# S5's rotation table begun right behind its angles, its powers doubled on POOL, the first scan two tiles earlier in the order

## The chip, the cores and the metric

The kernel runs on one core of a Trainium2 chip. The metric is the device time of one launch in microseconds. Before the change it is 912.65 us, the median of three runs (909.97 to 914.98).

The engines that matter here: TensorE (PE) does the matmuls, VectorE (DVE) and GpSimd (POOL) do elementwise work, ScalarE (ACT) does activations and copies, SyncE's queue (SP, SPq) issues all DMAs. Each engine takes its instructions strictly in the order in which the program lists them. An instruction that waits holds everything behind it on its engine.

## The reference, cut to what matters

A trunk of two layers over 512 positions of width 1024. Layer 0 is a hybrid: one input projection feeds S5 channel groups and Mamba-2 SSD heads, whose outputs are gated, concatenated and projected back. Layer 1 is a retention layer. The change is in layer 0's S5 part.

```python
def s5_mixer(u, lam_re, lam_im, log_dt, b, c, d_skip, glu_w, glu_b):   # 64 groups, 64 complex states, 16 channels
    dt = exp(log_dt); mag = exp(min(lam_re, -1e-4) * dt)
    ab = mag * (cos(lam_im * dt) + 1j * sin(lam_im * dt))       # one decay and one angle for each state
    coef = (ab - 1) / lam
    bb = coef * b
    # over all positions:  x[t] = ab * x[t-1] + bb @ u[t]
    y = real(c @ x) + d_skip * u
    y = gelu(y);  return y * sigmoid(y @ glu_w + glu_b)
# beside it, from the same projection: xbc -> silu(depthwise conv of 4 taps) -> chunked SSD scan, chunks of 128
# y = concat(y_s5 * silu(z_a), rmsnorm(y_ssd * silu(z_b))) @ w_out + residual
```

## The kernel before, in words

**Layout.** Activations stand transposed, channels on 128 partitions, the 512 positions along the free axis. A projection tile is 128 output channels: PE sums over 8 blocks of the input. Tiles before x3 use plain float32 (`mm1`, L214, or L249 for the first two). From x3 on a weight tile is split into a high and a low part (`split_w`: ACT copies the high part at L107, DVE subtracts to get the low part at L108), and PE makes three products for each block (`mm3`, L115 to L117). So each such tile needs DVE's L108 before its first L117. Tiles x0 to x11 are the SSD input: ACT L354 and three DVE instructions at L357 do the conv out of PSUM, ACT L359 the SiLU. Tiles u are S5's input, z the gates. The sums stand in three PSUM buffers, so a tile waits until the one three back has been read out.

**S5.** The recurrence is cut into blocks of 8 positions (64 blocks, `NK`). Four stages j = 0..3 hold 16 groups each.
- `s5_params` (order entry `q0`) works on [128, 64] parameters: `exp_parts` of log dt, then dt, lr, a second `exp_parts`, the angles `th` (L595 to L600), sine and cosine of half the angle (`sin_cos`), the first power `pw` (L607, L612), the coefficients `cf` (L613 to L628), powers 1 to 8 by three doublings on DVE (`cmul` at L634, six instructions each), `al` = powers times coefficients (L640), copies of the powers for the outputs (`pws`, ACT L649 and L651) and the DRAM copy `al_d` (L655). Last comes the **rotation table** `rot`: DVE makes six levels of angles and their sines and cosines (tile `s5lv`, L669 to L679), then POOL doubles the table from 1 to 64 columns (L682 to L691): seven complex products of six POOL instructions, at L534 to L539, with products in `s5rt` and sums in `rot`.
- `s5_setup` (also in `q0`) builds `bd` on POOL (`s5cm`, L716 and L717; `s5bd`, L720).
- `s5_state` (`g`) makes the input matrices from `al_d` and `b` (tiles `al`, `b`, `tm`; DVE, or POOL for the pairs in `POOL_P`, L742 to L746). `s5_scan` (`a`): 64 PE matmuls (L755), then on DVE a rotation into the scan frame (L767, L768, L770, reading `rot`), the scan itself (L772), and the rotation back (L775, L777, L782).
- `s5_kern` (`b`) makes output products O on POOL (L798 eight times and L802 four times for each j) from the powers, and stores them (`o_d`, L803). `s5_taps` (`k`) multiplies them by `bd` on PE (L814) and stores the taps. `s5_out` (`c`) gives the output.

**What sets the order.** `ORDER` is a list of stages written by hand: d steps, e decay, q S5 parameters, w the split of the input, x conv tiles, u and z projection tiles, s and t the SSD chunks, and l g a b k c for S5. At build time a planner gives every engine its order: among the instructions whose inputs are ready in its own estimate of time it takes the lowest priority number, and numbers rise in the order in which the program is traced, so in the order of `ORDER`. `rank(v)` overrides the number: -3,000,000 for the start of layer 0, -2,000,000 for weight splits (`rank_w`), -1,000,000 for work that reads PSUM out (`rank_e`). `issue_after(ins)` puts what is traced within it behind `ins` on that engine. Tiles take one of a fixed number of buffers of their tag (`m`: 20, `f`: 8); an instruction whose tile finds none free waits for the last reader of the tile that holds one.

Of the kernel before, what the change touches and what calls it, by code (L numbers as in the profile page):

```python
# [35 lines left out]
ORDER = """d0 x8 x10 x9 e0 x11 q0 x0 b0 x1 x2 w0 l0 g0 x3 x4 x5 x6 k0 b1 a0 x7 g1 s0 u2 u3 l1 t0 s1 z0 a1 z1 k1 b2 t1 s2 u4 c0 u5
# [12 lines left out]
def trunk_kernel(ctx: ExitStack, tc: tile.TileContext, a: dict, out: bass.AP):  # L49
# [481 lines left out]
    def cmul(eng, o, x, y, shape, name, conj_tmp):  # L531
        (orr, oi), (xr, xi), (yr, yi) = o, x, y
        t1, t2 = conj_tmp
        eng.tensor_tensor(t1, xr, yr, op=ALU.mult)  # L534
# [4 lines left out]
        eng.tensor_tensor(oi, t1, t2, op=ALU.add)  # L539

    def s5_params(pr):
        W = 64
# [27 lines left out]
        def sin_cos(hh, qq, zz, th, n):  # L570
            vec.tensor_scalar(hh[:, 0], th, 0.5, None, op0=ALU.mult)
            vec.scalar_tensor_tensor(n, hh[:, 0], -1.0, hh[:, 0], op0=ALU.mult, op1=ALU.max)
            vec.tensor_scalar(hh[:, 1], n, -1.0, 0.5 * math.pi, op0=ALU.mult, op1=ALU.add)
            vec.tensor_tensor(zz, hh, hh, op=ALU.mult)
            vec.tensor_scalar(qq, zz, 1.0 / math.factorial(13), None, op0=ALU.mult)
# [55 lines left out]
        for n_ in (1, 2, 4):  # L631
            base = pw[:, n_ - 1, :, :]
            sh_ = [P, n_, W]
            cmul(vec, (pw[:, n_:2 * n_, 0, :], pw[:, n_:2 * n_, 1, :]),  # L634
                 (pw[:, 0:n_, 0, :], pw[:, 0:n_, 1, :]),
                 (base[:, 0, :].unsqueeze(1).broadcast_to(sh_), base[:, 1, :].unsqueeze(1).broadcast_to(sh_)),
                 sh_, "pw", (cm1[:, 0:n_, :], cm2[:, 0:n_, :]))
# [2 lines left out]
        cmul(vec, (al[:, :, 0, :], al[:, :, 1, :]),  # L640
             (pw[:, :, 0, 32:64], pw[:, :, 1, 32:64]),
             (cf[:, 0, 32:64].unsqueeze(1).broadcast_to(sb), cf[:, 1, 32:64].unsqueeze(1).broadcast_to(sb)),
             sb, "al", (cm1[:, :, 0:32], cm2[:, :, 0:32]))
# [14 lines left out]
        vec.tensor_tensor(m8, mag[:, 0:32], mag[:, 0:32], op=ALU.mult)  # L658
        for _ in range(2):
            vec.tensor_tensor(m8, m8, m8, op=ALU.mult)  # L660
        rot = big("rot", [P, 2, 32, NK])
        pool.memset(rot[:, 0, :, 0:1], 1.0)
        pool.memset(rot[:, 1, :, 0:1], 0.0)
        lvs = t("m", "s5lv", n=384).rearrange("p (n i w) -> p n i w", i=2, w=32)
        NL = 6
        sl = [P, NL, 32]
        ang, cnt_, sc, q2 = (f(f"s5lv{i}", [P, 2, NL, 32]) for i in range(4))
        th_, n_ = ang[:, 0], cnt_[:, 0]
        for i in range(NL):  # L669
            vec.tensor_scalar(th_[:, i], th[:, 0:32], 8.0 * 2 ** i, None, op0=ALU.mult)  # L670
        vec.tensor_scalar(n_, th_, 0.5 / math.pi, MAGIC, op0=ALU.mult, op1=ALU.add)
        vec.tensor_scalar(n_, n_, MAGIC, None, op0=ALU.subtract)
        for cst in (TWO_PI_1, TWO_PI_2, TWO_PI_3):
            vec.scalar_tensor_tensor(th_, n_, -cst, th_, op0=ALU.mult, op1=ALU.add)
        sin_cos(sc, q2, cnt_, th_, n_)
        sh, ch = q2[:, 0], q2[:, 1]
        vec.scalar_tensor_tensor(lvs[:, :, 1], sh, 2.0, ch, op0=ALU.mult, op1=ALU.mult)  # L677
        vec.scalar_tensor_tensor(n_, sh, -2.0, sh, op0=ALU.mult, op1=ALU.mult)
        vec.tensor_scalar(lvs[:, :, 0], n_, 1.0, None, op0=ALU.add)  # L679
        n = 1  # L680
        rt = f("s5rt", [P, 2, 32, 16])
        while n < NK:  # L682
            lv = lvs[:, n.bit_length() - 1]
            for k0 in range(0, n, 16):
                nn = min(16, n - k0)
                sh = [P, 32, nn]
                cc, cs_ = (lv[:, i].unsqueeze(2).broadcast_to(sh) for i in range(2))
                xr, xi = (rot[:, i, :, k0:k0 + nn] for i in range(2))
                yr, yi = (rot[:, i, :, n + k0:n + k0 + nn] for i in range(2))
# [461 lines left out]
```

## Time and profile before

| what | value |
|---|---|
| median of three runs | 912.65 us (909.97 to 914.98) |
| profiled execution, device time | 915.33 us |
| its span, first to last instruction | 913.6 us |
| PE busy / granted clock, mean | 868.6 us (95%) / 0.975 |
| DVE busy | 542.5 us (59%) |
| ACT busy | 359.5 us (39%) |
| POOL busy | 229.3 us (25%) |

The span is what the trace covers; the device time has 1.7 us more around it. A busy PE isn't a PE at its peak, and a mean share says little of one stage: layer 0's early part, up to about 330 us, has other limits than the rest.

### The profile page before, as it was taken

How to read it: one execution, taken by the hardware profiler on the slowest of the kernel's cores; microseconds unless marked ns; L12 is line 12 of the kernel's file. 1: busy time of each engine (PE TensorE's matmuls, PEld its weight loads, DVE VectorE, ACT ScalarE, POOL GpSimd, SP SyncE). 2: the span in 40 equal slices, each digit the busy share in tenths (PEclk: the TensorE clock that was granted, in tenths of full speed). 3: DMA queues.
4: the chain of work that ended last, by engine and by line, in shares of the span. 5: the costliest groups of instructions: out<-in, count | busy, mean ns of one | idle time of the engine just before them, and what ended most of it. 6: DMA issues, size and time to landing. Idle time of an engine off the chain costs nothing.

```text
span 913.6 us, 11520 instructions
## 1 busy us (share of the span) xinstructions
PE 868.6 (95%) x4348; PEld 683.1 (75%) x4348; DVE 542.5 (59%) x922; ACT 359.5 (39%) x572; POOL 229.3 (25%) x187
## 2 busy tenths in 40 slices
PE   8999955989989899999999999999999999999996
PEld 4345744757768787888888888888888888888885
DVE  6978769894883466453444544655633644448445
ACT  4323344425216444433434244345411244254432
POOL 0069997170572500000013122201000303110020
PEclk9999977979999899999999999999999999999999
DMA  7386313756549636773543221221332221222322
GB/s 244 122 223 210 106 51 119 204 161 205 148 124 323 215 104 190 255 238 107 208 141 112 93 93 47 93 92 47 99 103 99 93 91 47 93 70 70 116 70 93
DMA packets 64184, 121.45 MB, mean 133 GB/s; under 512 B 18112, under 2 KB 28672, under 8 KB 64000
## 3 DMA queue, kind: packets, MB, share of 16 engines
q1 hardware_dynamic: 64128, 120.71, 41.2%
q8 instruction: 34, 0.56, 0.2%
q14 instruction: 22, 0.18, 0.1%
HBM read 103.61 MB, written 17.07 MB: 132 GB/s over the span
## 4 chain that ended last, share of the span: by engine, by line
PE 68%; DVE 12%; POOL 8%; DMA 5%; SPq 2%; issue 2%; ACT 1%; ACTq 0%; POOLq 0%; DVEq 0%
PE g L115 3%; PE qk L117 3%; PE qk L116 3%; PE g L117 3%; PE g L116 3%; PE qk L115 3%; PE v L930 3%; PE v L931 3%; PE v L929 3%; PE gl L116 2%; PE gl L117 2%; PE gl L115 2%; PE out L117 2%; PE oa L116 2%; PE oa L117 2%
## 5 line engine op out<-in xcount | busy, mean ns | idle before, releaser
L903 POOL TENSOR_TENSOR rt<-rt,ru 128x512 f32<-128x512 f32 x16 | 27.2, 1721 | 134.7 <-DVE ru L902 134.7
L972 POOL TENSOR_TENSOR os<-os,os 128x512 f32<-128x512 f32 x12 | 15.5, 1292 | 139.8 <-ACT os L970 106.9
L882 POOL TENSOR_TENSOR hs<-hs,hs 128x512 f32<-128x512 f32 x7 | 12.0, 1708 | 92.5 <-ACT hs L880 92.5
L798 POOL TENSOR_TENSOR O<-ct,s5pws 128x512 f32<-128x512 f32 x16 | 24.1, 1508 | 31.2 <-DMA ct<-in_s5c_dram 31.2
L405 ACT ACTIVATE dec<-dec,nacs 128x128 f32<-128x128 f32 x64 | 19.5, 388 | 29.3 <-DMA dec<-at_d 29.3
L902 DVE TENSOR_TENSOR ru<-qk,tab 128x512 f32<-128x512 f32 x16 | 10.9, 683 | 32.4 <-PE qk L117 32.4
L357 DVE SCALAR_TENSOR_TENSOR cva<-xbc,cvw,cva 128x511 f32<-128x511 f32 (+2 forms) x36 | 26.6, 740 | 4.3 <-ACT cva L354 4.0
L798 POOL TENSOR_TENSOR ot<-ct,s5pws 128x512 f32<-128x512 f32 x16 | 28.1, 1756 | 0.0
L802 POOL TENSOR_TENSOR O<-O,ot 128x512 f32<-128x512 f32 x16 | 27.3, 1736 | 0.0
L742 POOL TENSOR_TENSOR tm<-al,b 128x512 f32<-128x512 f32 x6 | 9.0, 1513 | 57.3 <-DMA b<-in_s5bP_dram 34.2
L461 POOL TENSOR_TENSOR za6r<-za6r,y 128x512 f32<-128x512 f32 x1 | 1.3, 1297 | 80.9 <-DMA h_d<-hb 80.9
L359 ACT ACTIVATE cva<-cva 128x512 f32<-128x512 f32 x12 | 7.6, 631 | 33.7 <-DVE cva L357 33.6
L1004 DVE TENSOR_TENSOR h<-h,out 128x512 f32<-128x512 f32 x8 | 5.5, 686 | 25.5 <-PE out L117 25.5
L1065 POOL TENSOR_TENSOR fin<-fin,fnw 128x512 f32<-128x512 f32 x4 | 5.1, 1301 | 58.7 <-ACT fq L1029 58.7
L535 POOL TENSOR_TENSOR s5rt<-rot,s5lv 128x512 f32<-128x512 f32 (+4 forms) x7 | 5.9, 837 | 50.7 <-DVE s5lv L677 50.7
L845 PE MATMUL Y<-T,U 128*64 128x128 f32 x128 | 17.4, 294 | 0.2 <-issue 0.2
L499 DVE TENSOR_TENSOR hb<-ob,hb 128x512 f32<-128x512 f32 x8 | 5.5, 689 | 20.1 <-PE ob L117 20.1
L528 DVE TENSOR_TENSOR h<-oa,h 128x512 f32<-128x512 f32 x8 | 5.5, 690 | 19.6 <-PE oa L117 19.6
L848 ACT ACTIVATE ysb<-Y 128x256 f32<-128x256 f32 x16 | 5.2, 379 | 30.2 <-PE Y L845 18.1
L844 PE MATMUL Y<-Or,X 128*64 128x128 f32 x64 | 13.7, 298 | 2.3 <-DMA Or<-o_d 2.3
L120 ACT ACTIVATE rh<-rt 128x512 fp32r<-128x512 f32 (+1 forms) x16 | 9.1, 577 | 16.9 <-POOL rt L903 16.9
L425 PE MATMUL y<-ident,yos 128*128 128x128 f32 x48 | 12.2, 339 | 3.8 <-DVE yos L399 3.8
(1726 smaller groups left out, 3012.4 us busy)
## 6 DMA issues: line engine op xcount, KB each, us to landing
al<-al_d SPq DMA_DIRECT2D x8, 512.0 KB
b<-in_s5bP_dram SPq DMA_DIRECT2D x8, 512.0 KB
dec<-at_d SPq DMA_DIRECT2D x8, 512.0 KB
o_d<-O SPq DMA_DIRECT2D x16, 256.0 KB
T<-kd SPq DMA_DIRECT2D x64, 64.0 KB
Or<-o_d SPq DMA_DIRECT2D x16, 256.0 KB
x<-in_xT_dram SPq DMA_DIRECT2D x8, 256.0 KB
u_d<-us SPq DMA_DIRECT2D x8, 256.0 KB
```

The lines of the kernel that those rows point to most:

```text
L115: pe.matmul(ps, wh[:, k, :], xh[k], start=start and i == 0, stop=False)
L116: pe.matmul(ps, wh[:, k, :], xl[k], start=False, stop=False)
L117: pe.matmul(ps, wl[:, k, :], xh[k], start=False, stop=stop and i == len(ks) - 1)
L357: vec.scalar_tensor_tensor(g[:, d:], ps[:, 0:SEQ - d], cvw[:, m, j:j + 1], g[:, d:], op0=ALU.mult, op1=ALU.add)
L405: act.activation(dec[:, i, :], dec[:, i, :], AF.Abs, bias=nacs[:, c, 8 * gr + i:8 * gr + i + 1])
L798: pool.tensor_tensor(x.rearrange("p (g k c) -> p g k c", g=4, c=16), ct[:, c, par, 4 * hf:4 * hf + 4].unsqueeze(2).broadcast_to(sh), pws[: ...
L802: pool.tensor_tensor(o, o, tm, op=ALU.add)
L845: pe.matmul(dst, U[:, 8 * par + 4 * hf + i, :], Tp[hf][:, 2 * i + par, :], start=False, stop=True)
L903: pool.tensor_tensor(t1, t1, t2, op=op)
L929: pe.matmul(ps[c], hh[kk][:, cs], wh[:, i, :], start=kk == 0, stop=False)
L930: pe.matmul(ps[c], hh[kk][:, cs], wl[:, i, :], start=False, stop=False)
L931: pe.matmul(ps[c], hl[kk][:, cs], wh[:, i, :], start=False, stop=kk == KD - 1)
```

## The change

The table's code is moved ahead of the coefficients into a function of its own, called as soon as the angles and the first power are written; its instructions are the same. The three doublings of the powers and `al` go from DVE to POOL, with rank -900,000. The first `exp_parts` gets rank -3,500,000. The products of `s5_kern` are put behind the table's last instruction on POOL. In `ORDER`, `b0` goes from before `x1` to behind `x4`, `a0` from behind `x6` to between `x5` and `x6`, and `k0 b1` behind `g1`. `sin_cos` takes the engine as an argument and is given DVE in both calls.

```diff
-ORDER = """d0 x8 x10 x9 e0 x11 q0 x0 b0 x1 x2 w0 l0 g0 x3 x4 x5 x6 k0 b1 a0 x7 g1 s0 u2 u3 ...
+ORDER = """d0 x8 x10 x9 e0 x11 q0 x0 x1 x2 w0 l0 g0 x3 x4 b0 x5 a0 x6 x7 g1 k0 b1 s0 u2 u3 ...
@@ s5_params
-        sf, em = exp_parts(pr[:, 2, :])
+        with rank(-3500000):
+            sf, em = exp_parts(pr[:, 2, :])
...
         vec.tensor_scalar(pw[:, 0, 0, :], nr, 1.0, None, op0=ALU.add)
+        def rotation():
+            m8 = sv.tile([P, 32], F32, name="s5m8")
...
+            rot = big("rot", [P, 2, 32, NK])
...
+            for i in range(NL):
+                vec.tensor_scalar(th_[:, i], th[:, 0:32], 8.0 * 2 ** i, None, op0=ALU.mult)
...
+            sin_cos(vec, sc, q2, cnt_, th_, n_)
...
+            while n < NK:
...
+                    last = cmul(pool, (yr, yi), (xr, xi), (cc, cs_), sh, "rot", (rt[:, 0, :, 0:nn], rt[:, 1, :, 0:nn]))
+                n *= 2
+            return m8, rot, last.ins
+
+        m8, rot, rot_last = rotation()
         den, t1, t2 = s(), s(), s()
...
-            cmul(vec, (pw[:, n_:2 * n_, 0, :], pw[:, n_:2 * n_, 1, :]),
+            with rank(-900000):
+                cmul(pool, (pw[:, n_:2 * n_, 0, :], pw[:, n_:2 * n_, 1, :]),
...
-        cmul(vec, (al[:, :, 0, :], al[:, :, 1, :]),
+        with rank(-900000):
+            cmul(pool, (al[:, :, 0, :], al[:, :, 1, :]),
...
-        m8 = sv.tile([P, 32], F32, name="s5m8")
...
-                cmul(pool, (yr, yi), (xr, xi), (cc, cs_), sh, "rot", (rt[:, 0, :, 0:nn], rt[:, 1, :, 0:nn]))
-            n *= 2
@@ s5_kern
-                for c, x in enumerate((o, tm)):
-                    pool.tensor_tensor(x.rearrange("p (g k c) -> p g k c", g=4, c=16),
...
+                with tc.issue_after(s5["rot_last"]):
+                    for c, x in enumerate((o, tm)):
+                        pool.tensor_tensor(x.rearrange("p (g k c) -> p g k c", g=4, c=16),
...
                 pool.tensor_tensor(o, o, tm, op=ALU.add)
```

## Rows read from the trace of the kernel before

**Rows 1.** Stretches: length, busy time of PE, PEld, DVE, ACT, POOL, granted clock, DMA.
```profile
101.00:124.30 23.30, 23.30 (x174) 18.75 (x172) 12.77 (x14) 6.64 (x10) 22.44 (x19) 1.00 0.29 94
124.30:161.00 36.70, 17.44 (x55) 12.53 (x55) 35.98 (x37) 19.68 (x40) 30.41 (x18) 0.72 0.32 101
...
127.80:138.00 10.20, 4.12 (x9) 2.88 (x10) 10.20 (x15) 8.32 (x24) 10.20 (x8) 0.50 0.01 2
...
148.30:158.50 10.20, 4.78 (x11) 3.79 (x12) 10.08 (x8) 1.53 (x3) 6.41 (x4) 0.50 0.35 114
```
**Rows 2.** Waits of PE, 0 to 330 us: total, times, longest.
```profile
PE z L117 <- DVE z0l L108: 7.8, 1, 7.8
PE u L115 <- DVE cva L357: 5.2, 1, 5.2
PE u L117 <- DVE u3l L108: 4.2, 1, 4.2
```
**Rows 3.** Waits of DVE, 84 to 161 us.
```profile
DVE gi L767 <- POOL rot L536: 4.2, 1, 4.2
DVE X L768 <- POOL rot L539: 2.8, 1, 2.8
...
DVE xbc7l L108 <- ACT xbc7h L107: 1.7, 1, 1.7
```
**Rows 4.** Wait of ACT at the second scan's mg, 84 to 161 us.
```profile
ACT mg L760 <- POOL s5rt L538: 12.3, 1, 12.3
```
**Rows 5.** POOL in order of time, the table's first and last instruction: start, duration.
```profile
52.76 0.35 POOL L535 TENSOR_TENSOR s5rt<-rot,s5lv 128x32 f32<-128x32 f32 x1 [50.71 <-DVE s5lv L677]
...
122.98 1.30 POOL L539 TENSOR_TENSOR rot<-s5rt 128x512 f32<-128x512 f32 x1
```
**Rows 6.** POOL's busy time on the table (tile rot), then on bd (tile s5cm).
```profile
50.00:125.00 75.00, 35.41 (x42) 1.00 0.55 166
...
50.00:95.00 45.00, 0.00 (x0) 13.14 (x16) 1.00 0.72 212
```
**Rows 7.** POOL's busy time on the output products, L798, then on L802.
```profile
50.00:125.00 75.00, 15.82 (x9) 1.00 0.55 166
...
50.00:125.00 75.00, 5.40 (x4) 1.00 0.55 166
```
**Rows 8.** POOL's busy time on the table's products of 64, 128 and 256 elements.
```profile
59.00:89.50 30.50, 2.75 (x6) 1.00 0.72 226
90.00:95.45 5.45, 3.35 (x6) 1.00 0.24 81
95.50:100.65 5.15, 4.88 (x6) 1.00 0.26 91
```
**Rows 9.** DVE in order of time: the first power, xn.
```profile
23.02 0.19 DVE L612 TENSOR_SCALAR s5pw<-s5scr 128x64 f32<-128x64 f32 x1
...
25.72 4.91 DVE L255 TENSOR_TENSOR xn<-x,rbc 128x512 f32<-128x512 f32 x8
```
**Rows 10.** DVE's and POOL's busy time on the table's levels (tile s5lv).
```profile
39.00:54.00 15.00, 8.07 (x25) 0.62 (x2) 1.00 0.54 147
```
**Rows 11.** DVE line 121, POOL idle, then busy: min/median/max ns, first to last start.
```profile
L121 DVE TENSOR_TENSOR xl<-xn,xh x4: 680/681/682, 32.9 to 34.7; 128x512 fp32r<-128x512 f32 x4
...
L121 DVE TENSOR_TENSOR xl<-xn,xh x4: 692/1213/1639, 78.2 to 85.7; 128x512 fp32r<-128x512 f32 x4
```
**Rows 12.** PE in order of time: dt, the last taps' matmuls, half the first scan's.
```profile
26.47 7.04 PE L294 MATMUL dt<-xn,dtw 128*16 128x512 f32 x16 [1.42 <-DVE xn L255]
...
107.46 1.09 PE L814 MATMUL K<-O,s5bd 128*32 128x128 f32 x24
...
114.39 1.90 PE L755 MATMUL S<-U,al 128*64 128x64 f32 x32
```
**Rows 13.** SP in order of time: a weight load.
```profile
93.75 0.33 SPq L98 DMA_DIRECT2D u2w<-in_w_u_dram  x1
```
**Rows 14.** ACT in order of time: that weight tile's first use.
```profile
108.09 1.04 ACT L107 ACTIVATE u2h<-u2w 128x1024 fp32r<-128x1024 f32 x1
```

More of the change, by code (lines that the diff above doesn't have):

```diff
@@ L35 @@
 VEC_X = ((0, 0), (1, 0), (0, 1), (1, 1))
[L36 removed]
+ORDER = """d0 x8 x10 x9 e0 x11 q0 x0 x1 x2 w0 l0 g0 x3 x4 b0 x5 a0 x6 x7 g1 k0 b1 s0 u2 u3 l1 t0 s1 z0 a1 z1 k1 b2 t1 s2 u4 c0 u5
  t2 l2 g2 s3 z2 a2 z3 k2 b3 t3 u6 c1 u7 z4 l3 g3 z5 n0 z6 a3 z7 c2 n1 z8 k3 r0 z9 z10 r1 c3 z11 p0 p1 z12 p2 z13 p3 o0 o1 z14
@@ L538, in cmul @@
         eng.tensor_tensor(t2, xi, yr, op=ALU.mult)
-        eng.tensor_tensor(oi, t1, t2, op=ALU.add)
+        return eng.tensor_tensor(oi, t1, t2, op=ALU.add)
     def s5_params(pr):
@@ L568, in exp_parts, with sin_cos @@
             return sf, em
[L570 to L575, printed above, removed]
+        def sin_cos(eng, hh, qq, zz, th, n):
+            eng.tensor_scalar(hh[:, 0], th, 0.5, None, op0=ALU.mult)
+            eng.scalar_tensor_tensor(n, hh[:, 0], -1.0, hh[:, 0], op0=ALU.mult, op1=ALU.max)
+            eng.tensor_scalar(hh[:, 1], n, -1.0, 0.5 * math.pi, op0=ALU.mult, op1=ALU.add)
+            eng.tensor_tensor(zz, hh, hh, op=ALU.mult)
+            eng.tensor_scalar(qq, zz, 1.0 / math.factorial(13), None, op0=ALU.mult)
             for k in (11, 9, 7, 5, 3):
                 sg = 1.0 if (k // 2) % 2 == 0 else -1.0
-                vec.scalar_tensor_tensor(qq, qq, sg / math.factorial(k), zz, op0=ALU.add, op1=ALU.mult)
-            vec.scalar_tensor_tensor(qq, qq, 1.0, hh, op0=ALU.add, op1=ALU.mult)
-        sf, em = exp_parts(pr[:, 2, :])
+                eng.scalar_tensor_tensor(qq, qq, sg / math.factorial(k), zz, op0=ALU.add, op1=ALU.mult)
+            eng.scalar_tensor_tensor(qq, qq, 1.0, hh, op0=ALU.add, op1=ALU.mult)
+        with rank(-3500000):
+            sf, em = exp_parts(pr[:, 2, :])
         dt = s()
@@ L601, in s5_params @@
         hh, zz, qq = (scr2[:, i].rearrange("p (i w) -> p i w", w=W) for i in range(3))
-        sin_cos(hh, qq, zz, th, n)
+        sin_cos(vec, hh, qq, zz, th, n)
         sh, ch = qq[:, 0], qq[:, 1]
@@ L612, in s5_params @@
         vec.tensor_scalar(pw[:, 0, 0, :], nr, 1.0, None, op0=ALU.add)
+        def rotation():
+            m8 = sv.tile([P, 32], F32, name="s5m8")
+            vec.tensor_tensor(m8, mag[:, 0:32], mag[:, 0:32], op=ALU.mult)
+            for _ in range(2):
+                vec.tensor_tensor(m8, m8, m8, op=ALU.mult)
+            rot = big("rot", [P, 2, 32, NK])
+            pool.memset(rot[:, 0, :, 0:1], 1.0)
+            pool.memset(rot[:, 1, :, 0:1], 0.0)
+            lvs = t("m", "s5lv", n=384).rearrange("p (n i w) -> p n i w", i=2, w=32)
+            NL = 6
+            sl = [P, NL, 32]
+            ang, cnt_, sc, q2 = (f(f"s5lv{i}", [P, 2, NL, 32]) for i in range(4))
+            th_, n_ = ang[:, 0], cnt_[:, 0]
+            for i in range(NL):
+                vec.tensor_scalar(th_[:, i], th[:, 0:32], 8.0 * 2 ** i, None, op0=ALU.mult)
+            vec.tensor_scalar(n_, th_, 0.5 / math.pi, MAGIC, op0=ALU.mult, op1=ALU.add)
+            vec.tensor_scalar(n_, n_, MAGIC, None, op0=ALU.subtract)
+            for cst in (TWO_PI_1, TWO_PI_2, TWO_PI_3):
+                vec.scalar_tensor_tensor(th_, n_, -cst, th_, op0=ALU.mult, op1=ALU.add)
+            sin_cos(vec, sc, q2, cnt_, th_, n_)
+            sh, ch = q2[:, 0], q2[:, 1]
+            vec.scalar_tensor_tensor(lvs[:, :, 1], sh, 2.0, ch, op0=ALU.mult, op1=ALU.mult)
+            vec.scalar_tensor_tensor(n_, sh, -2.0, sh, op0=ALU.mult, op1=ALU.mult)
+            vec.tensor_scalar(lvs[:, :, 0], n_, 1.0, None, op0=ALU.add)
+            n = 1
+            rt = f("s5rt", [P, 2, 32, 16])
+            while n < NK:
+                lv = lvs[:, n.bit_length() - 1]
+                for k0 in range(0, n, 16):
+                    nn = min(16, n - k0)
+                    sh = [P, 32, nn]
+                    cc, cs_ = (lv[:, i].unsqueeze(2).broadcast_to(sh) for i in range(2))
+                    xr, xi = (rot[:, i, :, k0:k0 + nn] for i in range(2))
+                    yr, yi = (rot[:, i, :, n + k0:n + k0 + nn] for i in range(2))
+                    last = cmul(pool, (yr, yi), (xr, xi), (cc, cs_), sh, "rot", (rt[:, 0, :, 0:nn], rt[:, 1, :, 0:nn]))
+                n *= 2
+            return m8, rot, last.ins
+        m8, rot, rot_last = rotation()
         den, t1, t2 = s(), s(), s()
@@ L633, in s5_params @@
             sh_ = [P, n_, W]
[L634 to L637 removed]
+            with rank(-900000):
+                cmul(pool, (pw[:, n_:2 * n_, 0, :], pw[:, n_:2 * n_, 1, :]),
+                     (pw[:, 0:n_, 0, :], pw[:, 0:n_, 1, :]),
+                     (base[:, 0, :].unsqueeze(1).broadcast_to(sh_), base[:, 1, :].unsqueeze(1).broadcast_to(sh_)),
+                     sh_, "pw", (cm1[:, 0:n_, :], cm2[:, 0:n_, :]))
         al = f("s5al", [P, 8, 2, 32])
         sb = [P, 8, 32]
[L640 to L643 removed]
+        with rank(-900000):
+            cmul(pool, (al[:, :, 0, :], al[:, :, 1, :]),
+                 (pw[:, :, 0, 32:64], pw[:, :, 1, 32:64]),
+                 (cf[:, 0, 32:64].unsqueeze(1).broadcast_to(sb), cf[:, 1, 32:64].unsqueeze(1).broadcast_to(sb)),
+                 sb, "al", (cm1[:, :, 0:32], cm2[:, :, 0:32]))
         pws = sv.tile([P, 2, 8, 2, 32], F32, name="s5pws")
@@ L656, in s5_params @@
                              al[64 * h + 8 * jp:64 * h + 8 * jp + 8].rearrange("p k c f -> p (k c) f"))
-        m8 = sv.tile([P, 32], F32, name="s5m8")
[L658 to L689, printed above, removed]
-                cmul(pool, (yr, yi), (xr, xi), (cc, cs_), sh, "rot", (rt[:, 0, :, 0:nn], rt[:, 1, :, 0:nn]))
-            n *= 2
-        return dict(pws=pws, al_d=al_d, cf=cf, m8=m8, rot=rot)
+        return dict(pws=pws, al_d=al_d, cf=cf, m8=m8, rot=rot, rot_last=rot_last)
     def s5_setup(s5):
```

6 lines of the change are left out of this document (3 added, 3 removed).

## The prediction, made before the kernel was run

> **What bounds the kernel now.** I read the page's slices first: PE is busy in 95% of the span and has its holes in layer 0, before about 330 us. The waits of PE there name the largest: 5.2, 4.2 and 7.8 us, all ended by DVE [rows 2]. A table of stretches puts a price on their place. From 101 to 124.3 us PE is never idle while DVE works 12.77 of 23.30 us; from 124.3 to 161 us DVE works 35.98 of 36.70 and PE only 17.44 [rows 1]. So PE loses 36.70 - 17.44 = 19.3 us in a stretch whose bound is DVE, right behind a stretch in which DVE idles for 23.30 - 12.77 = 10.5 us. The waits of DVE say why it idles: 4.2 and 2.8 us at L767 and L768, the first scan's products, for the rotation table on POOL, and 1.7 us twice for ACT's half of a weight split (one of the two stands) [rows 3]. ACT too stands 12.3 us, since mg needs the buffer of the table's levels [rows 4]. The reader should see one cause: the table ends at 122.98 + 1.30 = 124.3 [rows 5], and what DVE could not do before comes in one heap behind it. The table is late because POOL starts it at 52.8 [rows 5] and spends 71.5 us, only 35.4 of them on it; 13.1 go to bd [rows 6] and 15.1 + 5.4 to the first output products (of the 15.82 us of L798 the ninth, 0.76 us, is the next stage's) [rows 7].
>
> PE pays once more: behind these waits its granted clock is 0.50, the 1.2 GHz level, from 127.8 to 138.0 and from 148.3 to 158.5, where it is busy 4.12 and 4.78 us [rows 1]. At the 2.4 GHz level that work would take half: 2.1 and 2.4 us less.
>
> **The change part by part.**
>
> *The table earlier.* The table's 25 DVE instructions on its levels cost 8.07 us [rows 10] and can begin behind the angles, well before the first power at 23.0 [rows 9]. Until xn at 25.7 DVE has no idle time, but the doublings leave it and the coefficients step behind, which I estimate frees 3 us. Then come xn (to 30.6) [rows 9], the scaled inputs and splits; 5 us of levels remain, so POOL gets them at about 38. The bounds are 33.5 (all hidden before) and 52.8 (the planner leaves the levels where they are). The rank of the first exp_parts moves the chain by 2 us at most and is worth nothing by itself, since PE is busy with u1 meanwhile.
>
> *POOL's sum.* The powers are 24 instructions of the shapes of the table's own levels: 2.75 + 3.35 + 4.88 us, and 4.88 for al, 15.9 in all [rows 8]. The first 11 start with the first power at 23.2 [rows 9] and are over by about 34; al needs the coefficients and falls beside the table, say 4.9 us. The table's 35.4 with its gaps of 1.5 us then ends at 38 + 36.9 + 4.9 = 80 with bd behind it, at 93 with bd's 13.1 within it. Bounds: 33.5 + 36.9 = 70, and 52.8 + 36.9 + 4.9 + 13.1 = 108, or 119 if the first 11 us of powers also stand in front. The output products follow, 20.5 us: their end is 101 to 114.
>
> *The first scan.* Its 64 matmuls stood at 108.5 and 114.4 on PE [rows 12]; in front of x6 and x7 they come at about 95 to 104, an estimate: one to two tiles earlier, a tile being some 6 us here (from the taps' 108.5 to the scan's 114.4). The table is there by then, so DVE's two waits go: -7.0 us, each one microsecond off the DVE-bound stretch. The scan's work now also fills the two waits of 1.7 us: -3.4 (bounds 0 and -4.2, all that is left of the idle 11.25 us from 101 to 161). What is late next is DVE itself: its 48.75 us of work in that stretch, 12.77 + 35.98 [rows 1], stays. PE keeps 19.3 - 10.4 = 9 us of waits.
>
> *The clock.* With about half the waits gone I take back one of the two slow stretches: -2.4, bounds 0 and -4.5.
>
> *Powers on POOL.* DVE loses 24 small instructions, 6 us if one takes 0.25 (the first power, of the smallest size, takes 0.19 [rows 9]). It loses them before the convs, where PE's own dt and x tiles cover DVE: 0 us; without that cover, the 6. Against it, POOL now works beside xn, which feeds dt's matmuls. The row: a split of xn's size takes 0.681 us with POOL idle, 1.213 in the median with POOL busy [rows 11]. Eight times 0.53 would put xn's end at 34.9, and dt's last pair of matmuls (7.04 / 8 = 0.88 us) [rows 12] 2.3 us late. Bounds 0 and +2.3; I take +1.0, since POOL has only nine products left to run by then. The Trainium skill, in "SBUF — State Buffer", section "Who interferes with whom", speaks against this edit: a VectorE instruction with two SBUF inputs and a GpSimd one that reads SBUF exclude each other, and the later blocks fully. The slowest row, 1.639, agrees with a full block. By that rule the term would be the whole 2.3 and the sum 1.3 smaller.
>
> *Products held, order changed.* Behind the first held product stand the rest of stage 0's products, then the taps on PE and the stores on SP's queue. Before, PE ran the taps until 108.5 [rows 12] without a wait. Now k0 stands behind x7, at about 117 on PE (where the scan's matmuls ended before, 114.39 + 1.90 = 116.3 [rows 12]), with products there from 101 to 114: 0 us, bounds 0 and (119 + 20.5) - 117 = +22. The stores come as much later in a queue that also holds weight loads; those run 108.09 - 93.75 = 14 us ahead of their use [rows 13, 14], so I take 0 there.
>
> The sum: -7.0 - 3.4 - 2.4 + 1.0 = -11.8 us. The profiled execution took 915.33 us, 913.6 of it span and 1.7 around it, so it would take 903.5. It is 2.7 above the median; on the median I say 900.9, rounded 901.
>
> **The rivals.**
>
> *PE gets everything back.* If the planner puts PE's own needs (the splits, the last conv) ahead of scan work on DVE, the stretch becomes PE-bound: -19.3 - 4.5 + 1.0, so 890. For it: in 101 to 124.3 all of DVE's work, needs and some of the rest, is 12.77 us beside 23.3 of PE [rows 1], and the scan's last pieces may run later. Against it: DVE hardly idles for the 36.7 us behind, and its order is fixed from an estimate.
>
> *No change.* The table isn't the only thing late: PE stands for the taps, or DVE's queue for something else, as long as it does now. A taps wait of 12 us, products at 129, would do it: 912. For it: POOL carries 16 us more and has no slack in the sum's upper half. Against it: the sum has the products 15 us earlier.
>
> *Slower.* The levels stay where they are, powers and bd stand before the table, and it ends at 119. The scan then sits on DVE in front of x6's and x7's convs and holds them: 119 - 104 = 15 us, which PE feels from u2 on; products end at 139.5, and the taps, which these waits have pushed to about 132, hold PE another 7.5. That is 22.5 of waits, and of the 19.3 of now I would keep some 4 for DVE's heap, since DVE can work it off meanwhile: +7, and with xn +8, so 920. It decides at a table end of about 108, where products at 128.5 cost PE the 12 us just won. For it: the planner did leave the levels behind conv and dt work. Against it: DVE's powers, ahead of the levels now, are gone, and 20.5 us of products can no longer come between.
>
> **How the numbers follow.** Forecast 0.48 (895 to 907), PE gets everything back 0.17, no change 0.19, slower 0.16. A change of 0.5%, 4.6 us, is about what can be told from none here: faster lies below 908.1, slower above 917.2. Faster: nearly all of the first two, 0.65; same: the third and a little of the others, 0.21; slower: 0.14. The range of 889 to 917 leaves out the best part of the second case (0.06) and the fourth (0.14). The likeliest case's own range is 895 to 907.
>
> **What would show it.** The table's first product at about 38 and its last at 80 to 93; no wait of DVE for `rot` and none of ACT at mg; the powers on POOL from 23 to about 34 and xn over 4.9 us by at most 4; scan matmuls ahead of x6; PE's waits between 101 and 161 at about 9 us, all by DVE; one slow-clock stretch fewer; no PE wait at the taps. I am wrong if the table ends by 95 and PE still waits 15 us or more there, if PE waits for O at the taps, or if a loss as large appears past 161.

## The result, and the profile after

The change made the kernel slower: 925.83 us, the median of 4 runs (921.6 to 926.82), 1.0132 times the time before [1.0088, 1.0176]; the same kernel run again gave 925.75 and 1.0157 [1.0135, 1.0179]. The forecast was 901 (889 to 917). A trace is one execution: the one before took 915.33 us, and the medians of five later groups of runs of it, 109 in all, lay at 909.7 to 912.6. So medians say by how much, and traces where.

Two stretches of the changed kernel, which answer to the first two of [rows 1]; columns as there.

```profile
101.00:124.30 23.30, 18.26 (x113) 15.03 (x114) 23.30 (x24) 3.23 (x6) 23.30 (x15) 0.87 0.46 130
124.30:161.00 36.70, 27.05 (x123) 19.98 (x123) 35.02 (x39) 24.50 (x46) 26.00 (x17) 0.79 0.34 114
```

DVE now works 23.30 of 23.30 us where it had worked 12.77, and as long as before behind it: 58.3 us in place of 48.75. PE, which had been full up to 124.3, now loses time there. The waits of PE from 0 to 330 us, changed kernel, against [rows 2]:

```profile
PE Y L852 <- DMA Or<-o_d: 11.0, 4, 4.1
PE xbc L115 <- DVE cva L357: 7.0, 2, 3.5
PE z L117 <- DVE z0l L108: 4.0, 1, 4.0
PE z L115 <- DVE cva L357: 3.8, 1, 3.8
...
PE S L762 <- DVE al L753: 1.5, 1, 1.5
```

Of the old waits at u 0.5 us is left, and that at z0 has halved. New are those for the convs of x tiles. Those for the loads Or, all past 200 us, are 11.0 where the same view of before has 2.5.

POOL in order of time, changed kernel (start, duration): the table's first product, the first power, the last of al, the table's last, against [rows 5].

```profile
40.62 0.27 POOL L535 TENSOR_TENSOR s5rt<-rot,s5lv 128x32 f32<-128x32 f32 x1 [39.06 <-DVE s5lv L635]
...
41.80 0.29 POOL L534 TENSOR_TENSOR s5cm<-s5pw 128x64 f32<-128x64 f32 x1
...
75.03 0.72 POOL L539 TENSOR_TENSOR s5al<-s5cm,s5cm 128x256 f32<-128x256 f32 x1
...
100.06 2.14 POOL L539 TENSOR_TENSOR rot<-s5rt 128x512 f32<-128x512 f32 x1
```

The levels came in time and the table ends 22 us earlier, at 102.2. But POOL stood idle for 39 us, while the first power was ready at 23.9 (DVE, L613): the powers are queued behind the table's first product, step by step between its products. al is done at 75.8; on DVE it was done at 41.1. al goes through DRAM into the first stage's input matrices (P0). DVE in order of time, kernel before: P0's first and last product with the first pair of its second half between them, and the convs of x3 and x4.

```profile
64.55 0.93 DVE L742 TENSOR_TENSOR tm<-al,b 128x512 f32<-128x512 f32 x1
...
71.75 1.27 DVE L742 TENSOR_TENSOR tm<-al,b 128x512 f32<-128x512 f32 x2
...
76.99 0.68 DVE L746 TENSOR_TENSOR al<-al 128x512 f32<-128x512 f32 x1
...
93.64 2.30 DVE L357 SCALAR_TENSOR_TENSOR cva<-xbc,cvw,cva 128x511 f32<-128x511 f32 x3
...
99.25 2.30 DVE L357 SCALAR_TENSOR_TENSOR cva<-xbc,cvw,cva 128x511 f32<-128x511 f32 x3
```

P0 stood between the steps of convs there too (x11's took from 63.9 to 71.2), but among the plain tiles, and PE lost nothing from 54.7 to 124. The same in the changed kernel: the conv of x2, that of x3 with P0's second half (its first half began at 90.41), and that of x4.

```profile
87.35 0.73 DVE L357 SCALAR_TENSOR_TENSOR cva<-xbc,cvw,cva 128x511 f32<-128x511 f32 x1
...
92.92 0.73 DVE L357 SCALAR_TENSOR_TENSOR cva<-xbc,cvw,cva 128x510 f32<-128x510 f32 x1
...
97.52 0.73 DVE L357 SCALAR_TENSOR_TENSOR cva<-xbc,cvw,cva 128x509 f32<-128x509 f32 x1
...
100.98 0.73 DVE L357 SCALAR_TENSOR_TENSOR cva<-xbc,cvw,cva 128x511 f32<-128x511 f32 x1
101.64 2.62 DVE L749 TENSOR_TENSOR tm<-al,b 128x512 f32<-128x512 f32 x2
104.18 0.73 DVE L357 SCALAR_TENSOR_TENSOR cva<-xbc,cvw,cva 128x510 f32<-128x510 f32 x1
104.84 0.94 DVE L752 TENSOR_TENSOR al<-al,b 128x512 f32<-128x512 f32 x1
105.72 1.57 DVE L750 TENSOR_TENSOR tm<-tm 128x512 f32<-128x512 f32 x1
...
107.21 1.60 DVE L752 TENSOR_TENSOR al<-al,b 128x512 f32<-128x512 f32 x1
108.75 0.73 DVE L357 SCALAR_TENSOR_TENSOR cva<-xbc,cvw,cva 128x509 f32<-128x509 f32 x1
109.41 1.45 DVE L108 TENSOR_TENSOR xbc6l<-xbc6w,xbc6h 128x1024 fp32r<-128x1024 f32 x1
110.78 0.74 DVE L357 SCALAR_TENSOR_TENSOR cva<-xbc,cvw,cva 128x511 f32<-128x511 f32 x1
...
112.29 3.10 DVE L749 TENSOR_TENSOR tm<-al,b 128x512 f32<-128x512 f32 x2
...
120.40 2.28 DVE L108 TENSOR_TENSOR xbc7l<-xbc7w,xbc7h 128x1024 fp32r<-128x1024 f32 x1
122.60 1.39 DVE L357 SCALAR_TENSOR_TENSOR cva<-xbc,cvw,cva 128x509 f32<-128x509 f32 x2
```

A conv of three steps that took 2.3 us in one piece takes 10.9 (x2's) and 8.5 (x3's), since P0's products stand between the steps, and x6's weight split stands behind all of it. x4's takes 12.5, and there P0 has its last product only. The rest is the first five products of the second stage's input matrices (P1's half on DVE, from 112.29) and x7's split. P1 stood at 111.3 before and met x6's conv; now it is x4's that comes so late. PE has three PSUM buffers, so x5 waits for the conv of x2 and x7 for that of x4 (PE, changed kernel):

```profile
98.40 0.47 PE L115 MATMUL xbc<-xh,xbc5h 128*128 128x512 f32 x1 [3.53 <-DVE cva L357]
...
123.48 0.76 PE L115 MATMUL xbc<-xh,xbc7h 128*128 128x512 f32 x1 [3.46 <-DVE cva L357]
```

Around and after these two waits its granted clock was at the 1.2 GHz level (stretches, changed kernel):

```profile
98.80:105.60 6.80, 5.72 (x19) 4.25 (x18) 6.80 (x7) 2.31 (x4) 6.72 (x5) 0.50 0.74 219
122.70:129.50 6.80, 6.02 (x14) 4.79 (x15) 6.80 (x10) 2.52 (x4) 6.72 (x6) 0.50 0.61 193
```

Each came with a wait of 3.5 us in front, and at half speed cost about as much again: 5.72 / 2 and 6.02 / 2.

In what follows PE's loss in a stretch is the time it isn't busy plus its busy time times (1 - granted clock), summed over windows of 1 us. Of the changed kernel's span, 9.5 us longer, it places some 10: +3.4 from 84 to 161, where the sum had -12.8, +7.5 behind it and -0.7 before. The table has one trace of each kernel that follows, times in us; the two traces of the changed kernel differ by up to 1.9 in a column.

| kernel | al done | P0 on DVE | table done | PE's loss to 84 | 84 to 124 | 124 to 161 | past 161 | ratio to before |
|---|---|---|---|---|---|---|---|---|
| before | 41.1 | 64.6-77.7 | 124.3 | 5.2 | 0.0 | 23.8 | 22.2 | 1 |
| changed | 75.8 | 90.4-112.4 | 102.2 | 4.5 | 12.6 | 14.6 | 29.7 | 1.0132 |
| changed, again | 75.4 | 89.7-112.0 | 101.8 | 4.8 | 12.8 | 15.6 | 27.8 | 1.0157 |
| e1 | 63.3 | 74.9-93.8 | 90.2 | 11.5 | 14.8 | 7.7 | 14.5 | 1.0065 |
| e2 | 41.8 | 66.4-84.5 | 118.3 | 11.5 | 3.2 | 17.1 | 21.8 | 1.0062 |
| e3 | 75.5 | 90.2-112.2 | 102.0 | 5.6 | 12.5 | 15.2 | 22.1 | 1.0094 |
| e4 | 91.6 | 104.0-125.6 | 117.8 | 4.6 | 9.5 | 8.5 | 21.8 | 0.9990 |
| n3 | 75.6 | 100.7-124.5 | 100.9 | 5.6 | 6.5 | 14.9 | 16.8 | 0.9940 |
| n7 | 92.3 | 105.1-125.3 | 118.7 | 7.2 | 9.7 | 7.8 | 23.1 | 0.9970 |
| n8 | 63.6 | 105.2-122.4 | 88.1 | 9.3 | 0.0 | 11.1 | 23.4 | 0.9975 |
| n1 | 41.6 | 63.9-77.4 | 105.9 | 7.0 | 8.9 | 17.0 | 8.8 | 1.0002 |
| n2 | 41.5 | 64.4-77.2 | 106.1 | 7.0 | 11.9 | 15.4 | 21.1 | 1.0053 |
| e7 | 41.2 | 63.4-78.4 | 127.6 | 5.4 | 7.0 | 20.9 | 13.6 | 0.9954 |
| n6 | 40.7 | 63.0-76.5 | 106.8 | 5.1 | 7.6 | 5.3 | 31.2 | 1.0024 |
| e5 | 42.2 | 65.4-79.6 | 104.3 | 7.0 | 17.3 | 9.3 | 16.7 | 1.0030 |
| n10 | 42.1 | 65.3-79.5 | 106.2 | 7.5 | 4.0 | 13.5 | 23.1 | 1.0038 |
| n11 | 58.7 | 81.2-108.3 | 98.2 | 5.3 | 17.6 | 10.2 | 16.9 | 1.0069 |
| n12 | 58.5 | 81.0-108.2 | 98.0 | 6.2 | 16.7 | 10.0 | 23.7 | 1.0142 |

### The profile page after: what moved, and what is told of

Its sections match the earlier page's. It is cut to its first block, busy times and chain, and to the rows that moved or that the text cites. A ratio compares the mean times of both kernels' runs of the same rounds, so it can differ in the third digit from the quotient of the medians.

```text
span 923.1 us, 11534 instructions
## 1 busy us (share of the span) xinstructions
PE 875.5 (95%) x4348; PEld 688.7 (75%) x4348; DVE 543.3 (59%) x898; ACT 366.7 (40%) x578; POOL 236.6 (26%) x211
## 4 chain that ended last, share of the span: by engine, by line
PE 75%; DVE 9%; POOL 8%; DMA 3%; ACT 2%; issue 2%; SPq 0%; POOLq 0%; ACTq 0%; DVEq 0%
PE g L115 3%; PE qk L117 3%; PE qk L116 3%; PE g L117 3%; PE g L116 3%; PE qk L115 3%; PE z L117 3%; PE v L938 3%; PE v L939 3%; PE v L937 3%; PE z L115 3%; PE z L116 3%; PE ob L116 2%; PE ob L117 2%; PE ob L115 2%; PE gl L115 2%
## 5 line engine op out<-in xcount | busy, mean ns | idle before, releaser
L910 DVE TENSOR_TENSOR ru<-qk,tab 128x512 f32<-128x512 f32 x16 | 10.9, 684 | 32.5 <-PE qk L117 32.5
L749 POOL TENSOR_TENSOR tm<-al,b 128x512 f32<-128x512 f32 x6 | 10.0, 1685 | 57.1 <-PE z L117 32.1
L806 POOL TENSOR_TENSOR ot<-ct,s5pws 128x512 f32<-128x512 f32 x16 | 24.6, 1537 | 0.0
L852 PE MATMUL Y<-Or,X 128*64 128x128 f32 x64 | 14.7, 318 | 8.6 <-DMA Or<-o_d 8.6
L1073 POOL TENSOR_TENSOR fin<-fin,fnw 128x512 f32<-128x512 f32 x4 | 5.0, 1291 | 58.5 <-ACT fq L1037 58.5
L852 PE MATMUL Y<-Or,mg 128*64 128x128 f32 x64 | 15.1, 325 | 4.6 <-DMA Or<-o_d 4.6
L852 PEld LDWEIGHTS Y<-Or,X 128*64 128x64 f32 x64 | 8.5, 159 | 10.1 <-issue 10.1
L120 ACT ACTIVATE rh<-rt 128x512 fp32r<-128x512 f32 (+1 forms) x16 | 9.1, 577 | 16.9 <-POOL rt L911 16.9
```

What stands on the lines that cost most here:

```text
L852: pe.matmul(dst, X[par][:, 4 * hf + i, :], O[2 * hf + par][:, i], start=True, stop=False)
```

## The experiments

The first theory: al, made late by its place on POOL, puts P0 between the convs. The rivals: the new order, the hold on the output products, or powers on POOL by contention.

**The changed kernel again** (no edit).

> The changed kernel itself once more, for a second trace of it and its ratio on the same chip as the others: 921 to 927, ratio 1.010 to 1.016. In the second trace P0 again between the convs at 90 to 112 and about 12 us lost by PE in 84 to 124; the losses past 161 may differ by some us from the first trace (29.7), since executions of one kernel differ by up to 9 us.

925.75 us, 1.0157. Both traces lose 12.6 and 12.8 us from 84 to 124, and 61.5 and 61.0 in all up to 420, where the columns end. The loss belongs to the kernel and not to one execution.

**e1, powers and al back on DVE.**

```diff
-            with rank(-900000):
-                cmul(pool, (pw[:, n_:2 * n_, 0, :], ...
+            cmul(vec, (pw[:, n_:2 * n_, 0, :], ...
```

> The changed kernel with the three doublings and al back on DVE; the early table, the hold and the new order stay. Theory (late powers): after the change the first power product on POOL started at 41.8 behind the table's first and al ended at 75.8 (before: 41.1 on DVE), so the input matrices of the first pair (P0, DVE L749 to L753 there) moved from 64.6-77.6 to 90.4-112.3. With the powers on DVE al ends at about 45, P0 comes before 84 and DVE's work in 84 to 124 falls by about 12 us; the table loses the 15.9 us of powers on POOL and ends at 85 to 90. Time 900 to 908, ratio to before 0.985 to 0.995. Rival A (the new order costs it): taps, O1 and the second stage's stores stay late, PE waits for Or past 200 stay at 11 us, time 918 to 926. Rival B (the hold costs it): O0 ends earlier by 12 with the table, time 912 to 920.

916.44 us, 1.0065 [1.0044, 1.0086]: half the loss goes, not all, and the time lies in rival B's range. al came at 63.3 and not at 45, because on DVE too the powers start late:

```profile
41.34 0.21 DVE L534 TENSOR_TENSOR s5cm<-s5pw 128x64 f32<-128x64 f32 x1
```

That is 0.9 us behind the table's first product at 40.42, as on POOL it was 1.2 us behind it. So the place of the table in the program makes the powers late, whichever engine has them; n11 below shows that it is the table's products and not its levels. P0 fell at 74.9 to 93.8 and held the conv of x0, for which x3's matmuls waited 4.0 us. P1's half, from 102.7, then stood in front of a split of the input (4.2 us of PE).

**e2, powers and al on POOL and nothing else** (the diff of e1 the other way round, in the kernel before).

> The kernel before with the doublings and al on POOL and nothing else. The table's levels come late here (52.8), so the powers needn't stand behind the table. Theory: the powers run from about 23 on POOL, al ends at 45 to 50, P0 moves by less than 10 us into a stretch where DVE idles: time 909 to 917, ratio 0.997 to 1.004; any loss is xn and the splits slowed by POOL, at most 3 us. Rival C (powers on POOL cost by contention or by their slow instructions, wherever they stand): 918 to 926, as after the change.

917.53 us, 1.0062 [1.0042, 1.0083]. al is done at 41.8, as early as on DVE, and yet it costs: POOL works beside xn and the dt chain. xn in this kernel, against 4.91 us [rows 9]:

```profile
25.62 7.18 DVE L255 TENSOR_TENSOR xn<-x,rbc 128x512 f32<-128x512 f32 x8 [0.72 <-ACT rbc L178]
```

PE's loss up to 84 rises from 5.2 to 11.5. The time lies between the theory's range (to 917) and rival C's (from 918). The price of 3 us at most was too low, and what rival C names, POOL beside DVE, is seen in this kernel, but not in the changed one, where xn took 4.91 again because no power ran before 41.8.

**e3, the old order.**

```diff
-... q0 x0 x1 x2 w0 l0 g0 x3 x4 b0 x5 a0 x6 x7 g1 k0 b1 s0 ...
+... q0 x0 b0 x1 x2 w0 l0 g0 x3 x4 x5 x6 k0 b1 a0 x7 g1 s0 ...
```

> The changed kernel with the order list of before. Theory: powers are late here too (al at about 75), P0 late, so DVE's heap in 84 to 124 stays, and the first scan stands behind x6 again: 916 to 926. Rival A (the new order costs it, by taps, O1, ks1 and Or being later): Or waits fall back from 11.0 to about 2.5 us, time 905 to 914. Rival B (the hold): 918 to 930, since O0 is wanted earlier by the taps.

919.98 us, 1.0094 [1.0066, 1.0122], as the theory said, though rival B's range holds it too: 12.5 us are lost from 84 to 124 as in the changed kernel. The loss past 161 falls to 22.1, that of before, so this part needs the new order.

**e4, no hold on the output products.**

```diff
-                with tc.issue_after(s5["rot_last"]):
+                if True:
```

> The changed kernel without the hold on the output products. Theory: the hold is a small part; products slip in between the table's products, the table ends later (110 to 118), taps come no earlier than about 125: 922 to 930. Rival B (the hold costs it by holding O, taps and stores back): 908 to 916, Or waits under 5 us.

910.25 us, 0.9990 [0.9968, 1.0012]. The theory had 922 to 930. Rival B had it right in size and in its sign, Or waits under 5 us: past 161 they are 3.0, in the changed kernel 13.2. But PE doesn't wait at the taps in the changed kernel, and the trace shows one thing more: without the hold O's products push al to 91.6, and P0 then comes at 104, behind x4's conv. Both "P0's place" and "the hold" were left; the next run parts them.

**n3, P0 queued on DVE behind x4's conv, all else as changed.**

```diff
...
+        def g_(j):
+            if j:
+                return s5_state(s5, j)
+            with tc.issue_after(held[4]):     # x4's last conv step
+                s5_state(s5, j)
-... w0 l0 g0 x3 x4 b0 x5 ...
+... w0 l0 x3 x4 g0 b0 x5 ...
```

> The changed kernel with one thing moved: the first pair's input matrices (P0, at L749 to L753 after the change) are queued on DVE behind x4's conv; table, powers on POOL, hold and order stay (the fourth stage letter for P0 moves from before x3 to behind x4). After the change P0 sat at 90.4 to 112.3 between the steps of the convs, each tile's conv took about 10 us in place of 2.3, and PE lost 9.5 us of waits and 3.1 us by the slow clock in 84 to 124 (before: 0). Theory (P0, made late by al behind the table, breaks the convs): x3's to x5's convs run in 2.3 us each again, PE loses under 5 us in 84 to 124, the scan comes at about 130, total 911 to 919. Rival B (the hold costs it by holding O, taps and stores back): O ends at 121 and the Or waits past 200 stay as after, 920 to 927.

907.06 us, 0.9940 [0.9925, 0.9954]: 18.7 us less than the changed kernel, faster than the kernel before, and below the theory's 911 to 919. Table, powers, al and the hold stand where they stood (100.9, 75.6); the edit moved P0 alone, by 10 us to later, and P1's half on DVE followed it, from 112.3 to 122.0. DVE, this kernel:

```profile
92.99 2.31 DVE L357 SCALAR_TENSOR_TENSOR cva<-xbc,cvw,cva 128x511 f32<-128x511 f32 x3
...
98.51 2.31 DVE L357 SCALAR_TENSOR_TENSOR cva<-xbc,cvw,cva 128x511 f32<-128x511 f32 x3
100.74 2.23 DVE L755 TENSOR_TENSOR tm<-al,b 128x512 f32<-128x512 f32 x2
...
109.48 0.74 DVE L357 SCALAR_TENSOR_TENSOR cva<-xbc,cvw,cva 128x511 f32<-128x511 f32 x1
...
121.31 0.74 DVE L357 SCALAR_TENSOR_TENSOR cva<-xbc,cvw,cva 128x509 f32<-128x509 f32 x1
```

The convs of x2 to x4 are whole again. x5's, beside P0 now, takes 12.6 us, yet PE waits 0.3 us for it: by then the first scan's matmuls and x6 and x7 stand between. The waits of PE past 161, in this kernel, in the changed one and in the kernel before:

```profile
PE Y L858 <- DMA Or<-o_d: 2.9, 3, 1.4
```

```profile
PE Y L852 <- DMA Or<-o_d: 13.2, 6, 4.1
```

```profile
PE Y L844 <- DMA Or<-o_d: 3.3, 3, 1.5
```

By the traces 5.8 us are won from 84 to 161 and 12.9 behind it, and 1.1 lost before. So most of the gain lies past 161, which the theory had not counted. One of the Or waits there, on SP in the changed kernel:

```profile
201.08 0.56 SPq L829 DMA_DIRECT2D kd<-ks  x1
203.25 0.32 SPq L836 DMA_DIRECT2D Or<-o_d  x1
...
204.76 0.32 SPq L836 DMA_DIRECT2D Or<-o_d  x1
...
206.74 0.32 SPq L836 DMA_DIRECT2D Or<-o_d  x1
```

Three Or loads stand behind the store of the second stage's taps, which waits for DVE's ks at 198.59; PE was there at 202 and waited 4.09. With P0 moved the same store went out at 190.47 and the loads at 192.6 to 196.3. That they come together is shown, and by e3 that it takes the new order; which step between them carries it was not tried, and the other waits for Or, 9.1 us past 260, were not followed.

**n7, n3 without the hold** (both edits above).

> The changed kernel with P0 queued behind x4's conv (the one that gave 907.1) and without the hold on the output products. Theory: the hold mattered in the changed kernel mostly because it decided when al was done and so where P0 fell (75.8 with it, 91.6 without); with P0 tied behind x4's conv both give the same: 904 to 911. Rival B (the hold costs by itself): 895 to 902.

909.14 us, 0.9970 [0.9946, 0.9993]: with P0 tied, taking the hold away gains nothing. So in the changed kernel the hold cost through P0's place. The theory held, rival B fell.

**n8, n3 with powers and al on DVE.**

> The changed kernel with P0 queued behind x4's conv (the one that gave 907.1) and the powers and al back on DVE. Theory (what counts is P0's place, and powers among DVE's dt chain cost): al ends at 63 on DVE, the dt chain and with it the decay sums come 11 us later (PE lost 11.5 us up to 84 with the powers alone back on DVE, 5.6 here), table at 88; 907 to 914, no better than with the powers on POOL. Rival (work on POOL beside DVE is what costs): 897 to 903.

908.66 us, 0.9975 [0.9947, 1.0002]. With P0 tied, the engine of the powers matters little: POOL is no worse.

**e7, the new order alone; n2, the hold alone; n1, both**, in the kernel before.

```diff
# e7, n1: the new ORDER line; n2, n1: the table's last product kept, and
+                with tc.issue_after(s5["rot_last"]):
```

> The kernel before with the new order alone: the table ends at about 120 to 124 as before, the first scan's matmuls come ahead of x6, taps behind x7. Theory: DVE's scan products wait for the table with the same end, but now in front of x6's and x7's convs in DVE's queue where the planner put them there: 912 to 922, PE losses in 84 to 124 about 5 to 10 us. Rival A (the new order costs by later taps and stores): loss past 161 some 7 us above before's 22, 916 to 922. If the order is harmless: 908 to 913.

> The kernel before with the hold alone, old order. Table ends at about 104, output products at 124; in this order the taps stood at 108 on PE, so PE waits for them up to 16 us, part of it won back since the scan behind them finds the table ready. Theory: 908 to 918. Rival B (the hold is what costs the 12 us): 920 to 926.

> The kernel before with the hold on the output products and the new order, and nothing else: table, powers and al stay where they were on DVE and POOL (al at about 41, P0 at 64 to 78). The table starts at 52.8 as before and loses 20 us of output products from its middle, so it ends at about 104, as after the change. Theory: with P0 early, the 4.2 and 2.8 us waits for the table go and nothing takes their place; PE's losses from 84 to 161 fall from 24 to about 14 us, time 899 to 907. Rival B (the hold itself costs, by O at 124 and taps and stores behind it): 912 to 924, the loss past 161 some 7 us above before's 22.

The order alone gains: 908.51, 0.9954 [0.9941, 0.9968], in the range named for a harmless order (908 to 913); the theory and rival A had it slower. The hold alone costs: 917.62, 1.0053 [1.0030, 1.0076]. Both: 911.55, 1.0002 [0.9980, 1.0024], outside the theory's 899 to 907, although the table ends at 105.9 and no wait of the scan for `rot` is left. In its place stands this one (waits of DVE, 84 to 161, n1):

```profile
DVE tm L742 <- POOL rot L539: 9.5, 1, 9.5
```

The second stage's first product (P1) takes the buffer of the table's products, and stands in front of x6's weight split, for which PE waits 6.7 us.

**n6, n1 with P1's half on DVE queued behind x6's conv** (the edit of n3, with `if j != 1` and `held[6]`).

> The kernel before with the hold and the new order (as the one that gave 911.6), and the second stage's input matrices (P1, DVE's half) queued on DVE behind x6's conv. There DVE stood 9.5 us at P1's first product, in front of x6's weight split, for the last instruction of the table (tm takes the buffer of the table's products, s5rt), and PE lost 6.7 us at that split. Theory (the hold costs by this buffer wait): the wait goes, PE's losses from 84 to 161 fall from 26 to 15 to 19 us, 901 to 908. Rival (the hold costs by O, taps and stores): the time stays at 909 to 914.

913.44 us, 1.0024 [1.0006, 1.0043]: the buffer wait is gone and the loss from 84 to 161 falls to 12.9, below what was expected, but the time doesn't. PE waits for the hold's late products instead, inside that stretch (waits of PE, n6):

```profile
PE K L821 <- POOL O L809: 8.1, 4, 5.4
```

and loses 31.2 us past 161. The theory was right on the wait and wrong on the time.

**e5, the table queued behind al on POOL.**

```diff
+                    with tc.issue_after(al_last):
                         last = cmul(pool, (yr, yi), (xr, xi), ...
```

> The changed kernel with the table's products queued behind al's last product on POOL, so that the powers start at the first power (about 23), as the prediction had it, and the table after al. Everything else of the change stays. Theory: al ends at about 50, the table at 95 to 100, P0 comes at 58 to 75 as before; POOL beside xn and the dt chain slows both (xn took 7.18 us in place of 4.91 with the powers alone moved, and PE's loss up to 84 was 11.5 us in place of 5.2), so 6 us go there; the 12.6 us in 84 to 124 go away in part: 908 to 916. Rival (the early table costs by itself, wherever the powers stand): 918 to 926. The prediction's sum, if its only error was the powers' place: 899 to 905.

914.75 us, 1.0030 [1.0011, 1.0049]: 11 us less than the changed kernel. P0 is back at 65.4. But the levels, too, now come late (the first table product at 51), xn takes 7.18, and DVE waits 9.5 us for the table's buffer at P1, in front of x5's split (14.7 us of PE).

**n10, e5 with P1 held as in n6.**

> The changed kernel with the table queued behind al on POOL (the one that gave 914.8) and P1's half on DVE queued behind x6's conv. With the table behind al, PE's largest wait was 14.7 us at x5's weight split, behind DVE's 9.5 us at P1's first product for the buffer of the table's products. If the failed step of the prediction is the powers' place alone, this kernel has what the prediction assumed (powers at 23, P0 before 75, nothing in front of the convs) and its sum: 899 to 906. Rival (P0 early isn't enough: the hold's late products then stop PE at the taps, as 8.1 us with P1 held in the other kernel, and POOL beside the dt chain costs 2 to 6 us up to 84): 908 to 915.

915.00 us, 1.0038 [1.0015, 1.0060]. The rival was right: 4.0 us lost from 84 to 124, but 7.5 before it and 3.9 at the taps.

**n11, the table cut in two: levels early, products behind al; n12, the same with P1 held.**

```diff
-        m8, rot, rot_last = rotation()
+        m8, rot, lvs = rotation()            # levels only
...
+        rot_last = table(rot, lvs, al_last)  # products, traced and queued behind al
```

> The changed kernel with the table cut in two: its levels stay right behind the angles on DVE (40.6 after the change), its products on POOL are traced and queued behind al. So the powers start at the first power and the levels are early too, which is what the prediction assumed; with the table wholly behind al (the one that gave 914.8) the levels had slipped to 51.2. The prediction's sum, if the powers' place was its only failed step: powers over by 40, table from 45 to 95, P0 before 84, 899 to 906. Theory (the place of P0 decides): al ends at 45 to 50, P0 at 66 to 82 among the plain tiles' convs, PE loses under 6 us in 84 to 124; but xn takes 7.2 us and P1's first product meets the table's buffer: 904 to 911. Rival (POOL beside DVE up to 84 costs as much as the early table gains): 911 to 916.

> The same with P1's half on DVE queued behind x6's conv, so that it can't stand in front of x5's and x6's weight splits for the table's buffer. If the kernel with the cut table shows such a wait: 2 to 6 us faster than it, 900 to 907. If the table ends before P1's first product there (by about 92): the same time as it.

915.79 us, 1.0069 [1.0043, 1.0095], and 921.74, 1.0142 [1.0104, 1.0179]. The powers start at 24.07, but bd comes between them, al is done at 58.7, and P0 falls at 81 to 108: 17.6 us lost from 84 to 124. n11's time lies in the rival's range (911 to 916), but not by its mechanism, since PE's loss up to 84 is 5.3, against 5.2 before. It is one more case of P0 among the x tiles' DVE work: PE waits 8.6 us for splits of the input. DVE has no wait for the table's buffer in n11, so holding P1 should have changed nothing; that n12 is 6 us slower stays unexplained. Since the powers moved to 24 when the table's product buffer was taken behind theirs, their place in the changed kernel seems to come from the order in which buffers are handed out; no run changed that alone.

## Why the prediction was wrong

**Right.** The levels reached POOL at 40.6 (38 forecast, bounds 33.5 to 52.8), no wait for `rot` is left on DVE and none at mg on ACT, the scan's matmuls came at 99 to 114 (95 to 104), PE didn't wait at the taps, and the table, at 102.2, was 9 us later than the sum's upper end but within its bounds. The new order alone gained 0.46% (e7), but with the table ending at 127.6, so that isn't the gain the sum named.

**The step that failed** is in "POOL's sum": "The first 11 start with the first power at 23.2 [rows 9] and are over by about 34; al needs the coefficients and falls beside the table, say 4.9 us." The first began at 41.8, and al, priced by its time on POOL, was done at 75.8. The prediction asked who is queued behind the powers on POOL and not who reads them: P0, 12 products on DVE, is in none of its steps. It moved from among the plain tiles, where PE lost nothing, to 90.4 to 112.4, among the convs that PE waits for. [rows 1] leaves DVE room in part of that stretch, and there was time for P0, but not between the steps of a conv. That makes "its 48.75 us of work in that stretch, 12.77 + 35.98 [rows 1], stays" false too: it became 58.3, and PE stood idle 14.7 us from 101 to 161 where 9 was forecast. P0's 12 products took 15.3 us in place of 9.6 (2.62 for the pair of L749 against 2.43 and 1.27 for the two pairs in the kernel before), beside the table's and then the output products on POOL. That P0's place is what cost is shown by n3, whose edit moves P0 alone: -18.7 us. How much of it is P1's half, which moved along, was not parted: the second of the two waits of 3.5 us stood mostly behind P1.

The clock term failed with it. In place of one slow stretch fewer there were three at the 1.2 GHz level, 98.8 to 105.6, 122.7 to 129.5 and 150.0 to 160.2. PE was busy 15.9 us in them, so they cost 7.9 where the two of before cost 4.5.

The rival "Slower" had the mechanism, DVE work queued in front of x6's and x7's convs, but with the scan as the work and a table end of 108 as its point. The table was in time; P0, and P1 behind it, did it, and to the convs of x2 to x4.

**What it wouldn't have saved.** No run with early powers reached 895 to 907. In e5 and n10 the levels came at 51, in n11 P0 was late, so both assumptions never stood together, and it stays open whether they can. But each part that was put at 0 or little had a price. Powers that do start at 23 cost xn the whole upper bound (e2, e5): 7.18 - 4.91 = 2.3 us, where +1.0 was taken. With the dt chain behind it PE's loss up to 84 rose by 6.3 us in e2 and by 1.8 in e5. The Trainium skill, in "SBUF — State Buffer", section "Who interferes with whom", says that a VectorE instruction with two SBUF inputs contends with a GpSimd one that reads SBUF; these runs agree, by the 7.18 us. Whether the later one blocks fully, as the prediction says by the same section, no run here settles. The hold, put at 0 with a bound of +22, costs 0.5% alone. And P1's first product waits for the table's buffer where its place on DVE comes before the table's end: 9.5 us in n1 and e5, 10.6 in n2. The prediction did not look for it.

**Past 161** the prediction named a loss as its own sign of being wrong and priced none. The stores were put at 0 for weight loads; the loads that suffered were Or, at 13.2 us of PE's waits in place of 3.3. Against the forecast the stretch from 84 to 161 came out 16.2 us worse (+3.4 in place of -12.8), and what lies past 161 7.5 us worse.

## What to carry to other kernels

When a step changes its queue or its place, follow what it makes to the last reader, and look where that reader will then stand: here neither the engine that took the work nor the one that gave it lost, but a consumer, two queues on, fell among the steps of the critical tile. In a queue that fills every gap, work that becomes ready late goes into the gaps of what is urgent; tie it behind a named step (n3) and see whether later is better. Here a wait of the nearly full engine cost its length and, where its clock then fell, about as much again (3.5 us, then 2.9 to 3.0).

## What the runs showed of the hardware

DVE and POOL slow each other in both directions: while xn ran 7.18 us in place of 4.91, POOL's products of 128 elements took 0.78 to 0.92 us, against 0.43 just before it (e2):

```profile
25.29 0.43 POOL L534 TENSOR_TENSOR s5cm<-s5pw 128x128 f32<-128x128 f32 x1
25.68 0.92 POOL L535 TENSOR_TENSOR s5cm<-s5pw 128x128 f32<-128x128 f32 x1
```

Moving small work off DVE onto POOL beside such a stretch is no relief.
